# Decoder block on one core: low parts of three gate/up weight operands by a negated copy and an accumulating transfer

## The chip, the core and the metric

The kernel is one program on one NeuronCore of a Trainium2 chip. The core has five engines that run their own instruction streams in order and wait for each other by semaphores: TensorE (PE in the profile; its weight loads are PEld), VectorE (DVE), ScalarE (ACT), GpSimd (POOL) and SyncE (SP). SP, ACT and POOL can issue transfers (DMAs), which then run beside the engines. The metric is the device time of one execution in microseconds (us), smaller being better.

## What is computed

The reference is a decoder layer on an input of 1024 rows by 1024 channels in float32: a mixer (pooling and differential attention), then a gated feed-forward network. Only the feed-forward network matters here:

```python
u = rms_norm(h, ffn_pre_g)
f = silu(u @ w_ffn_gate) * (u @ w_ffn_up)      # 1024 x 2816, called gate/up here
h = h + rms_norm(f @ w_ffn_down, ffn_post_g)   # called down here
```

Two devices shape the kernel. First, each float32 matrix is split into a high part `hi`, which is its value rounded to the type float32r, and a low part `lo = a - hi`; a product is then three matmuls, `hi*hi + hi*lo + lo*hi`. Second, products are made in the manner of Strassen and Winograd: an operand is cut into quarters, sums and differences of the quarters are formed, and seven products of a quarter's size take the place of eight. The operands of the seven products on the weight side are called B11, T1, B21, T2, T3, B22 and T4.

## The kernel before

The program runs through the mixer's projections, attention, the output projection, gate/up and down. In gate/up the 2816 hidden channels are 22 blocks of 128. Blocks 0, 1 and their partners are done one by one; the rest are done as nine *pairs*, `kb` from 2 to 10, block `kb` with block `kb + 11`. Down follows, with `FP = 11` steps for each of its seven products.

**A pair.** `pair_weights(kb)` loads four raw weight tiles of 128x1024 float32 (gate and up, each for the upper and lower half of the channels: `g0`, `u0`, `g1`, `u1`), two transfers of 256 KB each, on SP. It forms T1, T2, T3, T4 in place by `diff` on DVE. Each of the seven operands is then split: `copy` on ACT casts the raw tile to `hi`, and `tt` on DVE makes `lo` as raw minus `hi` (`split`, called by `both`, lines 1418 and 1422 being the DVE and ACT instructions themselves). `outer` keeps an operand whole, `inner` (for B21 and T4) cuts it once more. `pair_products` runs the products in the order of the table `ORDER`: `P1a` is the first product for the pair's first block, `P5b` the fifth (T1) for its second, and `2.1` to `2.7` and `4.1` to `4.7` are the seven small products (128x256 matmuls) in which the second and the fourth product are made. P6 uses T2, P7 uses T3 and P3 uses B22. In a product the line 1920 is `hi*hi`, 1921 is `hi*lo` and 1922 is `lo*hi`, `lo` of the weights being first read in line 1922. ACT copies the results of products 1, 5 and 6 out of the accumulator banks, DVE adds later ones to them, ACT applies silu, DVE multiplies, and SP writes the results to memory (`fsd`).

**What sets the order.** The instructions of this stage aren't issued in the order of the code. `hidden` records them as tasks in a `Plan`, with a cost in us, a rank and the tiles that they read and write. PE's tasks are chained in the given order. `deadlines` gives the others a due time that follows from PE's. `schedule` then fills the engines one task after another by these costs, with limits on the tiles alive (16 of the kind `vr` for `hi` and `lo`, 8 of `vf` for raw tiles), and `emit` issues them in the order of their planned starts. A tile may be claimed by a new user when all users of the old one are done. So a change of one cost or one task can move many others, and the physical tile that a value lands in (its name in the profile: `v`, `Wl`, `Wh`, `F`) differs between versions. `room` says when a task can have the tiles that it needs. Each engine still runs its stream in order on the chip, whatever the plan's costs were.

Of the kernel before, what the change touches and what calls it, by code (L numbers as in the profile page):

```python
# [12 lines left out]
F32R = mybir.dt.float32r  # L13
AF = mybir.ActivationFunctionType
ALU = mybir.AluOpType

P = 128
# [4 lines left out]
HALF = 512  # L22
# [35 lines left out]
class Slot:  # L58


    def __init__(self, pool, make, kind=None, value=None, free_at=None):
        self.pool, self.make, self.kind, self.value = pool, make, kind, value
        self.free_at, self.live, self.left = free_at, value is not None or free_at is not None, 0
        self.log, self.phys, self.first = [], None, None

    def __call__(self):
        return self.value
# [9 lines left out]
class Plan:  # L77
# [84 lines left out]
        return None if s.kind == "own" else self.queues.get(s.kind if s.kind in self.queues else s.pool)  # L162

    def room(self, t):
        need = {}
        for s in t.needs:
            if s.live:
                continue
            q = self.queue(s)
            if q and s not in q[:1 + sum(not x.live and self.queue(x) is q for x in t.needs if x is not s)]:  # L170
                return INF
            if s.pool:
                n, extra = need.get((s.pool, None), (0, 0))
                need[s.pool, None] = n + 1, max(extra, self.own.get(s.pool, 0) if s.kind == "late" else RESERVE.get(s.kind, 0))
                if s.kind in LIMIT:
                    need[s.pool, s.kind] = need.get((s.pool, s.kind), (0, 0))[0] + 1, 0
        at = 0.0
        for (p, kind), (n, extra) in need.items():
            live = [s for s in self.pools[p] if kind is None or s.kind == kind]
            over = len(live) + n + extra - (CAPS[p] if kind is None else LIMIT[kind])  # L180
            if over > 0:
                times = sorted(INF if s.free_at is None else s.free_at for s in live)
                at = max(at, times[over - 1] if over <= len(times) else INF)
        return at

    def schedule(self, patience=None, begin=None):
        patience = patience or {}
        free = {e: (begin or {}).get(e, 0.0) for e in ("PE", "ACT", "DVE", "POOL", "SP")}
        waiting = {t: len(t.before) for t in self.tasks}
        open_ = {e: [] for e in free}  # L190
        dma_free, order, port = 0.0, [], {"DVE": 0.0, "POOL": 0.0}
        for t in self.tasks:
            if not waiting[t]:
                open_[t.engine].append((0.0, t))
        for _ in range(len(self.tasks)):
            best = None
            for e, ts in open_.items():
                f, first = free[e], INF
                cand = []
                for ready, t in ts:  # L200
                    at = max(f, ready, self.room(t), port["POOL" if e == "DVE" else "DVE"] if t.port else 0.0)
                    if at < INF:
                        cand.append((at, t.rank, t))
                        first = min(first, at)
                if not cand:
                    continue
                lim = first + patience.get(e, 0.0) + 1e-9
                at, rank, t = min((c for c in cand if c[0] <= lim), key=lambda c: (c[1], c[0]))
                if best is None or at < best[0]:
                    best = at, t  # L210
            if best is None:
                stuck = [(t.engine, t.rank, [s.pool for s in t.needs if not s.live]) for ts in open_.values() for _, t in ts[:6]]
                raise RuntimeError(f"stuck {stuck} { {p: len(v) for p, v in self.pools.items()} }")
            at, t = best
            e = t.engine
            for s in t.needs:
                if s.pool and not s.live:
                    live = self.pools[s.pool]
                    same = [x for x in live if x.kind == s.kind]
                    if s.kind in LIMIT and len(same) >= LIMIT[s.kind]:  # L220
                        live.remove(min((x for x in same if x.free_at is not None), key=lambda x: x.free_at))
                    elif len(live) >= CAPS[s.pool]:
                        old = min((x for x in live if x.free_at is not None), key=lambda x: x.free_at)
                        live.remove(old)
                        s.phys = old.phys
                    else:
                        s.phys = len(live)
                    live.append(s)
                    if s.kind == "own":
                        self.own[s.pool] -= 1  # L230
                    elif self.queue(s):
                        self.queue(s).remove(s)
                s.live = True
            t.start = at
            if e == "PE" and at > free[e] + 1e-6 and free[e] > 0:
                t.start = at = at + PE_RESTART
            t.end = t.landed = at + t.cost
            if t.port:
                port[e] = t.end
            free[e] = t.end - min(OVERLAP.get(e, 0.0), t.cost / 2)  # L240
            if t.size:
                dma_free = max(dma_free, t.end) + t.size / DMA_RATE if t.size > .01 else dma_free
                t.landed = (dma_free if t.size > .01 else t.end) + DMA_LATENCY
            for s in t.uses:
                s.left -= 1
                if s.pool and not s.left:
                    s.free_at = max(x.landed + self.hop(x, t) for x, _, _ in s.log)
            open_[e] = [(r, x) for r, x in open_[e] if x is not t]
            order.append(t)
            for x in t.after:  # L250
                waiting[x] -= 1
                if not waiting[x]:
                    ready = max(b.landed + self.hop(b, x) for b in x.before)
                    open_[x.engine].append((ready, x))
        self.order = sorted(order, key=lambda t: t.start)
        return max(t.end for t in self.tasks)
# [440 lines left out]
def act(n):  # L697
    return 0.145 + n / 1180
# [10 lines left out]
def mixer(pl, k):  # L709
# [663 lines left out]
    for s in (F, *(t for ts in U2.values() for t in ts), *(t for hi, lo, _ in W2.values() for t in (hi, lo))):  # L1373
# [5 lines left out]
FIRST = {"B21": 2, "T4": 3}  # L1379
ORDER = ("P1a", "4.4", "P1b", "P5a", "2.1", "2.5", "P5b", "2.6", "2.2", "P6a", "2.7", "2.3", "P6b", "2.4", "P7a", "P7b",  # L1380
         "4.1", "4.5", "P3a", "4.6", "4.2", "P3b", "4.7", "4.3")
OUTER = {"1": ("Y", "B11", "A11"), "5": ("X", "T1", "S1"), "6": ("Y", "T2", "S2"), "7": ("Y", "T3", "S3"), "3": ("X", "B22", "S4"),
         "4": ("Y", "T4", "A22")}
INNER = {"1": ("Y", "B11", "A11", 0, 0), "5": ("X", "T1", "S1", 1, 1), "6": ("Y", "T2", "S2", 1, 0), "2": ("Z", "B21", "A12", 0, 0),
         "7": ("Y", "T3", "S3", 1, 1), "3": ("X", "B22", "S4", 1, 0), "4": ("Y", "T4", "A22", 0, 1)}
WRAPPED = ("4.4",)
KEEP_LATE = 10.0


def hidden(pl, k):  # L1390
# [3 lines left out]
    V, A, G = (nc.vector, nc.scalar, nc.gpsimd) if k else (None, None, None)  # L1394
    f32 = k.f32 if k else None
    FP, HQ = NF // 2, HALF // 2
    clock = [0.0]

    def formed(v, dt, shape):
        letters = "abc"[:len(shape)]  # L1400
        return v.rearrange(f"p ({' '.join(letters)}) -> p {' '.join(letters)}", **dict(zip(letters, shape)))

    def v4(dt, *shape):
        s = pl.tile("vr" if dt == F32R else "vf", None)
        s.make = lambda: formed(k.place(s.pool, s.phys), dt, shape)
        return s
# [10 lines left out]
    def tt(o, a, b, op, n, r, w, rank=1e5):  # L1417
        return pl.op("DVE", dve(n), lambda: V.tensor_tensor(out=o(), in0=a(), in1=b(), op=op), r=r, w=w, rank=rank,  # L1418
                     port=all(x.pool not in BANKS for x in slots(r, w)))

    def copy(o, a, n, r, w, rank=1e5, claim=()):
        return pl.op("ACT", act(n), lambda: A.copy(o(), a()), r=r, w=w, rank=rank, claim=claim)  # L1422
# [16 lines left out]
    for names in (("B11", "B21"), ("T1", "T3"), ("T2", "T4"), ("B22",)):  # L1439
        both = [pl.given("vr", k.W[names[0]][j]() if k else 0) for j in range(2)]  # L1440
# [24 lines left out]
    def keep_hidden(kb, q, behind=None):  # L1465
# [6 lines left out]
        def gp(o, a, b, op):  # L1472
            tt(q[o][0], q[a][0], q[b][0], op, HALF, [q[a][1], q[b][1]], [q[o][1]], clock[0] + KEEP_LATE)

# [115 lines left out]
    def pair_weights(kb):  # L1590
# [9 lines left out]
        def both(raw):  # L1600
            hi, lo = v4(F32R, 2, 4, P), v4(F32R, 2, 4, P)
            split(hi, lo, raw, 2 * HALF, [raw], [hi], [lo], claim=[lo])
            return hi, lo

        def outer(n, raw):
            hi, lo = both(raw)
            W[n] = [(hi, lo, e) for e in range(2)]

        def diff(o, a, b):
# [57 lines left out]
    def pair_products(kb, W, q, tail):  # L1667
# [9 lines left out]
        def outer(n, e):  # L1677
            o, w, a = OUTER[n]
            s, key, v = acc[o][e]
# [40 lines left out]
            if len(done) == 26 or (not deep["4"] and "P4b" in done):  # L1720
                keep_hidden(kb, q)

        order = ORDER
        if not deep["4"]:
            order = [x for x in order if x[0] != "4"] + ["P4a", "P4b"]
        for x in order:
# [661 lines left out]
```

## Time and profile before

| | |
|---|---|
| median of 3 runs | 1236.37 us (1236.11 to 1236.63) |
| the profiled execution, device time | 1236.7 us |
| its span, from the first to the last instruction | 1234.8 us |
| ACT busy, share of the span | 606.1 us, 49% |
| POOL busy, share of the span | 59.5 us, 5% |
| DMA bytes moved | 194.43 MB, mean 157 GB/s |

The profiled execution is 0.3 us above the median of the three runs, and 1.9 us of its time lie around its span. The page gives the busy time of each engine, forty slices of the span, the DMA queues, the chain of work that ended last, and the costliest groups of instructions. In a group's row stand the line, the engine, the operation, what it writes and reads, the count, the total busy time and the mean of one in ns, and then the engine's idle time just before, with what ended it. In the timeline, a row is start (us), duration (us), engine, line, operation, tiles, shape and count.

### The profile page before, as it was taken

The numbers are of one execution on the slowest core, as the hardware profiler recorded it, in microseconds if no ns is written. First come the engines' busy times: TensorE is split into PE (matmuls) and PEld (weight loads), VectorE is DVE, ScalarE is ACT, GpSimd is POOL, SyncE is SP. The second block draws the span as 40 slices with busy tenths as digits, with TensorE's granted clock in tenths as the row PEclk, the third lists the DMA queues.
The fourth block names the chain that finished last, engine by engine and source line by source line (L and its number), as shares of the span: only waits on it lengthen the run. The fifth ranks groups of instructions, "written<-read, shape, count | busy, mean of one in ns | idle before, by whom it ended". The sixth has DMA issues, their size and how long they took to land.

```text
span 1234.8 us, 16572 instructions
## 1 busy us (share of the span) xinstructions
PE 1225.1 (99%) x6166; PEld 1042.0 (84%) x6166; DVE 929.2 (75%) x1533; ACT 606.1 (49%) x1098; POOL 59.5 (5%) x64
## 2 busy tenths in 40 slices
PE   9999999999999999999999999999999999999997
PEld 8888888888899998888888888888888888888886
DVE  6986784534599888885877978778878788765666
ACT  8643444443588773454643434434434443644542
POOL 1000000000201110010000000000000000000222
PEclk9999999999999999999999999999999999999999
DMA  9665246323783027672424443223432299533336
GB/s 374 240 194 188 105 158 221 125 80 120 286 327 137 18 85 257 210 267 77 147 97 124 119 128 101 71 94 120 128 128 89 66 319 316 181 103 94 88 101 213
DMA packets 139153, 194.43 MB, mean 157 GB/s; under 512 B 9024, under 2 KB 83520, under 8 KB 138048
## 3 DMA queue, kind: packets, MB, share of 16 engines
q1 hardware_dynamic: 132256, 172.26, 42.1%
q10 hardware_dynamic: 6816, 21.11, 4.4%
q8 instruction: 48, 0.79, 0.3%
q14 instruction: 33, 0.27, 0.1%
HBM read 131.73 MB, written 61.60 MB: 157 GB/s over the span
## 4 chain that ended last, share of the span: by engine, by line
PE 96%; DMA 2%; ACT 1%; DVE 0%; SPq 0%; issue 0%; POOLq 0%; DVEq 0%; ACTq 0%
PE Y L1920 9%; PE Y L1921 9%; PE Y L1922 9%; PE X L1920 5%; PE X L1921 5%; PE X L1922 5%; PE Yd L1921 3%; PE Yd L1922 3%; PE Yd L1920 3%; PE s L731 3%; PE o L731 3%; PE qk L563 3%; PE wo L1920 2%; PE wo L1922 2%; PE wo L1921 2%; PE branch L1920 2%
## 5 line engine op out<-in xcount | busy, mean ns | idle before, releaser
L1827 DVE TENSOR_TENSOR w_op<-wd,w_op 128x512 fp32r<-128x512 f32 x72 | 52.2, 725 | 48.1 <-ACT w_op L1875 48.1
L1418 DVE TENSOR_TENSOR v<-v,v 128x1024 fp32r<-128x1024 f32 (+4 forms) x79 | 73.6, 936 | 9.1 <-ACT v L1422 7.8
L1875 ACT CAST w_op<-wd 128x512 fp32r<-128x512 f32 x72 | 44.8, 623 | 68.0 <-PE Yd L1922 32.1
L1922 PE MATMUL Y<-S_hi,Wl 128*128 128x512 f32 x200 | 77.9, 390 | 0.0
L1922 PE MATMUL X<-S_hi,Wl 128*128 128x512 f32 x200 | 77.8, 389 | 0.0
L1920 PE MATMUL Yd<-w_op,s_op 128*128 128x512 f32 x156 | 60.7, 389 | 0.0
L1921 PE MATMUL Yd<-w_op,s_op 128*128 128x512 f32 x156 | 60.7, 389 | 0.0
L1922 PE MATMUL Yd<-w_op,s_op 128*128 128x512 f32 x156 | 60.7, 389 | 0.0
L1422 ACT CAST v<-v 128x1024 fp32r<-128x1024 f32 (+2 forms) x52 | 42.0, 818 | 36.3 <-PE X L1921 23.7
L1827 DVE TENSOR_TENSOR s_op<-s_raw,s_op 128x512 fp32r<-128x512 f32 x69 | 53.9, 781 | 7.1 <-ACT s_op L1875 7.1
L1875 ACT CAST s_op<-s_raw 128x512 fp32r<-128x512 f32 x69 | 42.6, 617 | 29.6 <-DMA s_raw<-fsd 24.0
L1920 PE MATMUL Y<-A_hi,Wh 128*128 128x512 f32 x144 | 56.2, 390 | 0.0
L1921 PE MATMUL Y<-A_lo,Wh 128*128 128x512 f32 x144 | 56.2, 390 | 0.0
L921 DVE CUSTOM_DVE_ANT_0 E<-s,negd 128x1024 f32<-128x1024 f32 (+7 forms) x64 | 47.4, 748 | 11.4 <-PE s L731 11.3
L1920 PE MATMUL X<-S_hi,Wh 128*128 128x512 f32 x136 | 53.2, 391 | 0.0
L1920 PE MATMUL Y<-S_hi,Wh 128*128 128x512 f32 x136 | 53.1, 390 | 0.0
L1921 PE MATMUL Y<-S_lo,Wh 128*128 128x512 f32 x136 | 53.0, 390 | 0.0
L927 ACT ACTIVATE E<-E,nm 128x1024 f32<-128x1024 f32 (+7 forms) x64 | 49.6, 776 | 6.9 <-DVE nm L921 6.7
L1922 PE MATMUL Y<-A_hi,Wl 128*128 128x512 f32 x136 | 52.9, 389 | 0.0
L1921 PE MATMUL X<-S_lo,Wh 128*128 128x512 f32 x136 | 52.9, 389 | 0.0
L1920 PE MATMUL wo<-woh,mh 128*128 128x512 f32 x128 | 50.5, 394 | 0.0
L1922 PE MATMUL wo<-woh,ml 128*128 128x512 f32 x128 | 49.9, 390 | 0.0
(515 smaller groups left out, 3735.6 us busy)
## 6 DMA issues: line engine op xcount, KB each, us to landing
s_raw<-fsd SPq DMA_DIRECT2D x31, 512.0 KB, 3.7
fsd<-v SPq DMA_DIRECT2D x56, 256.0 KB, 3.5
w_raw<-in_w_in_dram SPq DMA_DIRECT2D x24, 512.0 KB, 4.1
wd<-in_w_ffn_down_dram SPq DMA_DIRECT2D x44, 256.0 KB, 5.2
sgs<-sgd SPq DMA_DIRECT2D x16, 512.0 KB, 8.6
sgd<-g_st ACTq DMA_DIRECT2D x14, 512.0 KB, 4.1
v<-in_w_ffn_up_dram SPq DMA_DIRECT2D x28, 256.0 KB, 4.5
v<-in_w_ffn_gate_dram SPq DMA_DIRECT2D x26, 256.0 KB, 3.4
```

Of the source, the lines that this page charges most:

```text
L563: nc.tensor.matmul(o()[:, cs], l, r, start=first and kk == 2 * kh and j == 0, stop=last and kk == 2 * kh + 1 and j == len(todo) - 1, skip_ ...
L731: nc.tensor.matmul(o, l, r, start=start, stop=stop, skip_group_check=skip)
L921: V.tensor_tensor_reduce(out=view[m]().rearrange("p (j w) -> p j w", j=nj), in0=sc()[:, :nj, :w], in1=negd()[:, S - L:S].rearrange("p (j w ...
L927: A.activation(view[m](), view[m](), AF.Exp, bias=nm()[:, m:m + 1], scale=-1.0, accum_out=sums()[:, m:m + 1])
L1418: return pl.op("DVE", dve(n), lambda: V.tensor_tensor(out=o(), in0=a(), in1=b(), op=op), r=r, w=w, rank=rank, port=all(x.pool not in BANKS ...
L1422: return pl.op("ACT", act(n), lambda: A.copy(o(), a()), r=r, w=w, rank=rank, claim=claim)
L1827: nc.vector.tensor_tensor(out=o, in0=a, in1=f32(hi), op=ALU.subtract)
L1875: nc.scalar.copy(hi, a)
L1920: nc.tensor.matmul(o, ah, bh, start=start, stop=False, skip_group_check=goes_on)
L1921: nc.tensor.matmul(o, ah, bl, start=False, stop=False, skip_group_check=goes_on)
L1922: nc.tensor.matmul(o, al, bh, start=False, stop=stop, skip_group_check=goes_on)
```

## The change

Three things are changed.

1. For the operands B22, T2 and T3 of each pair, `outer` no longer calls `both`. ACT casts raw to `hi` as before. ACT then writes `-hi` into the tile of `lo` (`A.mul` by -1), and POOL issues a transfer from the raw tile to the tile of `lo` that adds to what is there (`accum_op=ALU.add`), so `lo` becomes raw minus `hi`. DVE's subtraction for the three operands goes. B11, T1, B21 and T4 are made as before.
2. The last pair (`kb == FP - 1`) has an order of its own, `ORDER_LAST`: `4.7` stands ahead of `P3b`.
3. In the planner a tile remembers when it was granted (`since`), and a task that uses a granted tile isn't planned ahead of that time.

```diff
-        self.log, self.phys, self.first = [], None, None
+        self.log, self.phys, self.first, self.since = [], None, None, 0.0
...
     def room(self, t):
-        need = {}
+        need, at = {}, 0.0
         for s in t.needs:
             if s.live:
+                at = max(at, s.since)
                 continue
...
-        at = 0.0
         for (p, kind), (n, extra) in need.items():
...
-                s.live = True
+                if not s.live:
+                    s.live, s.since = True, at
...
+ORDER_LAST = (*ORDER[:-3], "4.7", "P3b", "4.3")
...
+SHARED = ("B22", "T2", "T3")
...
         def outer(n, raw):
-            hi, lo = both(raw)
+            if n in SHARED:
+                hi, lo = v4(F32R, 2, 4, P), v4(F32R, 2, 4, P)
+                copy(hi, raw, 2 * HALF, [raw], [hi], claim=[lo])
+                pl.op("ACT", act(2 * HALF), lambda: A.mul(lo(), f32(hi()), -1.0), r=[hi], w=[lo], rank=1e5)
+                pl.op("POOL", 1.0, lambda: G.dma_start(lo(), raw(), accum_op=ALU.add), r=[raw], w=[lo], rank=1e5, size=1.0)
+            else:
+                hi, lo = both(raw)
             W[n] = [(hi, lo, e) for e in range(2)]
...
-        order = ORDER
+        order = ORDER if kb < FP - 1 else ORDER_LAST
```

The streams of all engines are the same up to the first pairs; from there to the end of the pairs they differ. PE has the same 6166 matmuls.

**First place: ACT in the pair kb = 4.** Before, from the copy of P1a's result out of its bank (`COPY v_6073<-Y_6864`) on, with T2's cast (`Wl_5959`), T3's cast (`Wl_5890`) and the two copies of the fifth product (`p_`):

```order
L1422 COPY v_6073<-Y_6864 128x512
L1422 CAST v_6189<-v_6070 128x1024
L1429 ACTIVATE v_6145<-v_6145 128x512
L1422 CAST Wl_5959<-F_5749 128x1024
L1422 CAST v_6098<-v_6017 128x512
L1422 COPY v_6073<-Y_6895 128x512
L1422 CAST v_6098<-v_6017 128x256
L1422 COPY p_1171_6947<-X_6916 128x512
L1422 CAST Wl_5890<-v_6167 128x1024
L1422 COPY p_1174_6995<-X_6916 128x512
L1422 COPY u_1175_7022<-Y_6864 128x512
```

Now, in the same pair, the lines being nine or so higher; `L1612` is the negated copy, of T2 (`Wh_5960`), T3 (`v_6051`) and B22 (`v_6076`):

```order
L1612 ACTIVATE Wh_5960<-Wl_5959 128x1024
L1432 ACTIVATE v_6017<-v_6017 128x512
L1425 COPY F_5749<-Y_6870 128x512
L1425 CAST Wl_5941<-v_6017 128x1024
L1432 ACTIVATE v_6017<-v_6017 128x512
L1425 CAST v_6075<-v_6070 128x1024
L1425 COPY F_5749<-Y_6904 128x512
L1612 ACTIVATE v_6051<-v_6075 128x1024
L1425 COPY p_1171_6956<-X_6924 128x512
L1425 CAST Wl_5890<-F_5749 128x1024
L1425 COPY p_1174_6997<-X_6924 128x512
L1612 ACTIVATE v_6076<-Wl_5890 128x1024
```

T2's operand now stands ahead of the copy of P1a, T3's ahead of P5a's copy (`p_1171`), and B22's just behind P5b's (`p_1174`); before, T3's cast stood behind P5a's copy and B22's behind the first copy of the sixth product. POOL, which had nothing in this stage, issues the transfers, three to a pair in the order T2, T3, B22; those of this pair and the next begin with:

```order
L1613 DMA Wh_5960<-v_6073 128x1024
L1613 DMA v_6051<-v_6070 128x1024
L1613 DMA v_6076<-F_5749 128x1024
L1613 DMA Wh_5924<-v_6017 128x1024
L1613 DMA Wh_5942<-v_6073 128x1024
```

**Second place: who takes the raw tiles over.** T2's raw tile in this pair is `v_6073` and T3's is `v_6070`. SP now loads the next pair's `up` weights into them, with the writes of results (`fsd`) between:

```order
L1435 DMA v_6073<-in_w_ffn_up_dram 128x4x128
L1435 DMA fsd<-v_6167 128x512
L1435 DMA v_6073<-in_w_ffn_up_dram 128x4x128
L1435 DMA fsd<-v_6167 128x512
L1435 DMA fsd<-v_6017 128x512
L1435 DMA v_6070<-in_w_ffn_up_dram 128x4x128 x2
L1435 DMA v_6167<-in_w_ffn_gate_dram 128x4x128 x2
```

DVE then subtracts the two (`v_6073<-v_6070,v_6073`, the next pair's T3), and behind that stand the last quarter of T4 of this pair, the addition of `2.4` (`Yi_6948`), T4's `lo` (`Wh_5960<-v_6145,Wl_5959`), P7a's addition and B11's `lo` of the next pair:

```order
L1421 TENSOR_TENSOR v_6073<-v_6070,v_6073 128x1024
L1421 TENSOR_TENSOR v_6145<-v_6145 128x256
L1421 TENSOR_TENSOR F_5749<-F_5749,Yi_6948 128x256
L1421 TENSOR_TENSOR v_6145<-v_6145 128x256
L1421 TENSOR_TENSOR Wh_5960<-v_6145,Wl_5959 128x1024
L1421 TENSOR_TENSOR p_1171_6956<-Y_6870,p_1171_6956 128x512
```

So a raw tile is handed on to a load when the accumulating transfer out of it has landed, where before it was handed on at the end of DVE's subtraction.

**Third place: PE in the last pair.** Before, `4.2` (`Zi`) was followed by P3b (`X`):

```order
L1921 MATMUL Zi_8971<-A_hi_5653,v_6098 128x256
L1922 MATMUL Zi_8971<-A_hi_5653,v_6097 128x256
L1920 MATMUL X_8740<-S_hi_5816,v_6075 128x512
L1921 MATMUL X_8740<-S_lo_5852,v_6075 128x512
L1922 MATMUL X_8740<-S_hi_5816,Wh_5942 128x512
```

Now it is followed by two matmuls of down (`Yd`) and by `4.7` (`Yi`), behind which P3b stands:

```order
L1930 MATMUL Zi_8998<-A_lo_5666,Wh_5891 128x256
L1931 MATMUL Zi_8998<-A_hi_5653,v_6098 128x256
L1929 MATMUL Yd_9070<-Wh_5924,Wl_5890 128x512
L1930 MATMUL Yd_9070<-Wh_5924,Wl_5890 128x512
L1929 MATMUL Yi_8957<-v_6097,v_6076 128x256
L1930 MATMUL Yi_8957<-v_6097,v_6076 128x256
L1931 MATMUL Yi_8957<-v_6097,v_6188 128x256
```

`4.7` adds to the bank that `4.6` used, so it has to wait until DVE has added `4.6`'s result; P3b, 12 matmuls, no longer stands between the two.

## The prediction

> **What bounds the kernel now.** I read the page first: the span, the busy times, and the chain of work that ended last.
>
> ```profile
> span 1234.8 us, 16572 instructions
> PE 1225.1 (99%) x6166; PEld 1042.0 (84%) x6166; DVE 929.2 (75%) x1533; ACT 606.1 (49%) x1098; POOL 59.5 (5%) x64
> PE 96%; DMA 2%; ACT 1%; DVE 0%; SPq 0%; issue 0%; POOLq 0%; DVEq 0%; ACTq 0%
> ```
>
> PE is busy 1225.1 of 1234.8 us and makes 96% of the chain; the two shares agree. All that any change of the other engines can take away is 9.7 us of idle PE, wherever it lies. So the next view is the busy time by stretches: the products before the pairs, the pairs, and from there to the last matmul.
>
> ```profile
> core 0: us, PE busy (x) PEld busy (x) DVE busy (x) ACT busy (x) POOL busy (x), PEclk, DMA share, GB/s
> 615.00:715.00 100.00, 100.00 (x463) 83.58 (x462) 79.57 (x113) 43.92 (x65) 0.00 (x0) 1.00 0.36 114
> 715.00:1015.00 300.00, 300.00 (x1627) 260.62 (x1626) 246.16 (x403) 126.89 (x193) 0.00 (x0) 1.00 0.38 124
> 1015.00:1228.00 213.00, 213.00 (x949) 176.69 (x949) 151.61 (x240) 98.38 (x189) 22.68 (x19) 1.00 0.51 160
> ```
>
> From 615 to 1228 us PE isn't idle at all, at a granted clock of 1.00. DVE is busy 246 of 300 us in the pairs: high, but below 300, and the reader should see that PE is full beside it. Then the list of PE's waits over the whole span:
>
> ```profile
> PE qk L563 <- ACT A_hi L479: 1.6, 3, 0.8
> PE warm L339 <- POOL ident masks.py:199: 1.4, 1, 1.4
> PE branch L1920 <- DVE sgs L734: 0.3, 1, 0.3
> ```
>
> It has three entries, 3.3 us in all, and none is of the gate/up products (lines 1920 to 1922 with X, Y, Z, Xi, Yi, Zi). In the stage that is changed there is no PE wait to remove. A busy share hides small gaps, since a matmul's end is modelled; but the quoted starts below follow each other at 0.23 us, without a hole.
>
> **What is removed.** Nine pairs lose three subtractions each, 27 on DVE; ACT gains 27 passes over 128x1024. The rows of such instructions, by shape, in the pairs:
>
> ```profile
> L1418 DVE TENSOR_TENSOR Wl<-v,Wl 128x1024 fp32r<-128x1024 f32 x10 | 12.2, 1218 | 0.0
> L1422 ACT CAST v<-v 128x1024 fp32r<-128x1024 f32 x21 | 22.0, 1050 | 8.7 <-PE X L1922 3.3 <-PE Y L1921 3.0 <-PE Xi L1922 0.8
> ```
>
> DVE: 27 x 1.22 = 32.9 us less, 246 to about 213 of 300 us. On the path it is worth 0: PE waited for no DVE instruction here, so what is late next is PE itself, as before. ACT: the negated copy isn't in the trace; the cast of the same tile (1.05 us) is the nearest row, bounded below by nothing and above by twice that. 27 x 1.05 = 28.4 us more, 127 to about 155 of 300. It is covered by ACT's idle half, but the place counts, since each copy stands ahead of or behind a copy out of a bank. The rows of the pair kb = 4:
>
> ```profile
> 758.93 0.59 ACT L1422 COPY v<-Y 128x512 f32<-128x512 f32 x1 [1.16 <-PE Y L1922]
> 765.11 0.59 ACT L1422 COPY p<-X 128x512 f32<-128x512 f32 x1 [1.66 <-PE X L1922]
> 770.02 0.58 ACT L1422 COPY p<-X 128x512 f32<-128x512 f32 x1
> ...
> 771.00 0.39 PE L1922 MATMUL Y<-S_hi,Wh 128*128 128x512 f32 x1
> 778.64 0.39 PE L1922 MATMUL Y<-S_hi,Wl 128*128 128x512 f32 x1
> 784.35 0.28 PE L1920 MATMUL Xi<-A_hi,v 128*128 128x256 f32 x1
> 785.54 0.39 PE L1922 MATMUL X<-S_hi,Wh 128*128 128x512 f32 x1
> ```
>
> Ahead of P1a's copy ACT was idle for 1.16 us and ahead of P5a's for 1.66, so a pass of 1.05 fits; were P1a's copy late by 1 us, nobody would see it, since its bank is next used by P6a, 12 us on. I take 0.
>
> **What is added: a transfer in the operand's path.** By the order now, the copies for T2, T3 and B22 are done by P1a's copy (758.93), by P5a's (765.11), and 1.05 us behind the end of P5b's (770.02 + 0.58 + 1.05 = 771.65). The first matmuls that read these low parts are the line 1922 rows of P6a (771.00), P7a (778.64) and P3a (785.54). So the windows, from the start on POOL to the need, are **12.1, 13.5 and 13.9 us**. The trace has no accumulating transfer and no transfer from POOL. The nearest rows, by size and by engine:
>
> ```profile
> s_raw<-fsd SPq DMA_DIRECT2D x31, 512.0 KB, 3.7
> vd<-v_st ACTq DMA_DIRECT2D x4, 1024.0 KB, 4.4
> V<-vd SPq DMA_DIRECT2D x4, 1024.0 KB, 10.6
> v<-in_w_ffn_up_dram SPq DMA_DIRECT2D x28, 256.0 KB, 4.5
> ...
> L855 POOL TENSOR_TENSOR wb_lo<-wb_raw,wb_hi 128x1024 fp32r<-128x1024 f32 x4 | 10.1, 2524 | 60.3 <-ACT wb_hi L853 60.3
> L1091 POOL TENSOR_TENSOR rstd<-ms,mhalf 128x1 f32<-128x1 f32 x16 | 9.6, 599 | 128.4 <-DVE ms L1095 118.0 <-DVE ms L1099 10.4
> ```
>
> It writes 512 KB and reads two operands of 512 KB. From below: POOL's smallest instruction, 0.6, and a 512 KB landing, 3.7, in all 4.3 us. From above: POOL over a whole 128x1024 tile, 2.5, and the slowest landing of 1,024 KB, 10.6, in all 13.1. I take 1.5 for POOL's part, midway, and 4.4 for the landing, because the row `vd<-v_st` also reads 1,024 KB out of the core's own memory and runs at a moderate load, as here (DMA share 0.38): **about 6 us**. That is half the shortest window, so PE doesn't wait: 0 us. POOL has nothing else in this stage, so nothing is queued behind its waits but the next transfer, 6 us later.
>
> **What is moved: the raw tile is released later.** Before, the next load could follow DVE's subtraction; now it follows the landing. The place that decides is T3's raw tile: landing, then two loads on SP, then DVE's difference for the next pair, and in DVE's queue behind that T4's low part, which `4.5` (784.35) needs. The rows for the terms that aren't quoted yet:
>
> ```profile
> 799.40 0.94 SPq L1432 DMA_DIRECT2D F<-in_w_ffn_gate_dram  x2
> ...
> 1012.45 0.28 PE L1920 MATMUL Yi<-Wh,v 128*128 128x256 f32 x1
> 1013.37 0.42 DVE L1418 TENSOR_TENSOR v<-v,Yi 128x256 f32<-128x256 f32 x1
> ```
>
> Issue 0.9, landing 4.5, difference 1.22, three small DVE instructions 3 x 0.42, T4's cast 1.05 and subtraction 1.22 make 10.15 us. T3's transfer starts by 765.11, and 784.35 - 765.11 - 10.15 = **9.1 us** is what it may take. Six is less: 0 us. SP's other work behind those loads is writes of results, which nobody waits for in this stage.
>
> **The last pair.** Between `4.6` and `4.7`, which adds to the same bank, now stand `4.2` (0.72) and two matmuls of down (0.45), 1.17 us in place of 3.4. DVE's addition of `4.6` ended at 1013.79, 0.62 after the product's last issue slot (1012.45 + 0.72). If DVE is in a 0.7 us instruction just then, PE waits some 0.2 us. I take 0; at most 0.7.
>
> **The sum.** 1236.7 (the profiled execution, 1234.8 of span and 1.9 around it) - 0 + 0 + 0 + 0 = 1236.7, and for the median, which lay 0.3 lower, **1236.4 us**.
>
> **The rivals.**
>
> *The raw tiles come late (slower).* If the transfer takes more than 9.1 us from POOL's start, DVE stands at the next pair's difference, and each of the eight pairs that have a next one loses the excess, since T3's start is tied to PE's own progress by P5a. At 10.5 us that is 8 x 1.4 = 11 us, 1248; at the upper bound of 13.1, 8 x 4.0 = 32, 1268. For it: three transfers a pair are added to a DMA share of 0.38, and 10.6 us is on record for 1,024 KB. Against it: 4.4 is on record too. 9%.
>
> *POOL can't start while DVE runs (slower).* DVE's work in the pairs comes in long stretches without idle time, for example between these two rows, of which each tells the idle time before it:
>
> ```profile
> 798.14 1.22 DVE L1418 TENSOR_TENSOR v<-F,v 128x1024 fp32r<-128x1024 f32 x1 [0.63 <-ACT v L1422]
> 807.45 0.42 DVE L1418 TENSOR_TENSOR v<-v,Yi 128x256 f32<-128x256 f32 x1 [0.64 <-PE Yi L1922]
> ```
>
> That stretch is 807.45 - 0.64 - 798.14 = 8.7 us. If POOL had to sit it out, 6 us would become 14.7, the raw tiles would be 5.6 us late, and 8 x 5.6 = 45 us would give 1281. If POOL gets its turn after one instruction (1.22 us), 6 becomes 7.2 and nothing is seen. Nothing in the trace speaks for it, since POOL was idle in the pairs. 6%. The Trainium skill, "SBUF — State Buffer", section "SBUF: two separate sides", warns of this case: a transfer issued from POOL has its descriptors written by GpSimd's cores, which DVE's two-port operations lock out of the port pair they share. By that rule the time would be between 1236 and 1281, by how many instructions it waits; by the rows alone it is 1236.4. The same section ties the lock to two-port modes, and "Advanced Engine Details and Errata", section "Instruction Support", lists none for tensor_tensor, DVE's only kind of instruction in the quoted rows; no run here shows a POOL transfer beside DVE yet.
>
> *One early wait (no measurable change).* In the first deep pairs DVE forms the quarters of A22 in a raw tile that T3 of kb = 3 gives up, with additions for PE queued behind. Such a wait happens once; between 8 and 9.1 us of transfer it costs about 1 us, 1237.5. 7%.
>
> *Faster.* The change does relieve DVE, but its gain needs a PE wait to remove. Inside the pairs there is none, and outside nothing is moved. More than 2.5 us could only come from matmuls that run quicker, of which no row gives a sign. 3%, at 1233.
>
> **How the numbers follow.** The forecast, no change, has 75%: 1235.8 to 1237.0, the spread of the runs before (0.5 us) and some tenths for the last pair. A measurement of this kernel can tell about 0.2%, 2.5 us, from no change. Same: 75 + 7 and 1 from the mildest late tiles, 83%. Slower: the rest of the two rivals, 14%. Faster: 3%. The range runs from 1235.4 to 1239.5: it takes in the forecast, the early wait and late tiles up to 0.4 us a pair, and leaves out some 13% above and 3% below. The rivals above reach far, but with little chance.
>
> **What would show it.** DVE's busy time lower by about 33 us and ACT's higher by about 28 say that the exchange is as costed. 27 transfers from POOL with about 6 us from issue to landing, and an empty list of PE waits between 615 and 1228 us, say that it is hidden. PE waits on Y or X at line 1922 would mean that the transfer itself is late; on Xi or Yi at line 1920, with DVE waiting for a `v<-in_w_ffn_up` load or for a POOL transfer, that the raw tiles are. POOL instructions of more than 3 us would speak for the rival of DVE's stretches. The prediction is wrong if the transfer takes over 9 us in the steady pairs, or if PE's matmuls change their pace.

## The result, and the profile after

| | before | changed |
|---|---|---|
| median | 1236.30 us (4 runs, 1236.11 to 1236.63) | 1252.88 us (4 runs, 1251.30 to 1255.63) |
| ratio, 95% interval | 1 | 1.0136, 1.0116 to 1.0157 |
| profiled execution, its span | 1236.7, 1234.8 us | 1254.09, 1252.3 us |

The changed kernel is slower by 16.6 us. The forecast of 1236.4 us was wrong, and so was its range, which ended at 1239.5. In the rows of the changed kernel the lines of DVE, ACT and SP (1418, 1422, 1429, 1432 before) are three higher, not nine as said above; 1920 to 1922 are 1929 to 1931. The page of the changed kernel has, for the rows shown of before:

```profile
span 1252.3 us, 16690 instructions
...
PE 1231.2 (98%) x6166; PEld 1045.6 (83%) x6166; DVE 897.7 (72%) x1506; ACT 635.3 (51%) x1125; POOL 83.2 (7%) x91
...
PE 89%; DVE 4%; DMA 4%; issue 2%; ACT 1%; SPq 0%; DVEq 0%; POOLq 0%; ACTq 0%
...
L1421 DVE TENSOR_TENSOR v<-v,v 128x1024 f32<-128x1024 f32 (+3 forms) x43 | 43.8, 1023 | 22.7 <-DMA v<-in_w_ffn_up_dram 9.6
...
L1929 PE MATMUL X<-S_hi,Wl 128*128 128x512 f32 x100 | 40.8, 408 | 9.7 <-DVE u L1421 9.7
```

The exchange is as costed: DVE 31.5 us less, ACT 29.2 more. But the span grew by 17.5 us: PE's idle time rose from 9.7 to 21.1 us, by 11.4, and its busy time, for the same 6166 matmuls, by 6.1. The chain that ended last now has DVE in it with 4% (0% before) and DMA with 4% (2%). The last two rows say where: DVE stands before the differences of weights (`v<-v,v`) for loads, and PE stands before P3b (`X`, line 1929 now) for DVE's addition into `u`. The stretches and PE's waits say the same:

```profile
core 0: us, PE busy (x) PEld busy (x) DVE busy (x) ACT busy (x) POOL busy (x), PEclk, DMA share, GB/s
615.00:715.00 100.00, 100.00 (x463) 83.58 (x462) 74.95 (x108) 47.54 (x67) 3.71 (x4) 1.00 0.47 134
715.00:1015.00 300.00, 287.93 (x1530) 248.03 (x1529) 201.67 (x348) 140.68 (x197) 20.15 (x23) 0.99 0.54 141
```

```profile
PE X L1929 <- DVE u L1421: 11.1, 7, 2.1
...
PE Xi L1931 <- DVE Wh L1421: 0.8, 1, 0.8
PE Xi L1929 <- ACT Wl L1425: 0.2, 1, 0.2
```

Columns: who waited for whom, us in total, times, longest. Seven waits of P3b, 11.1 us in all, once in each of the pairs kb = 3 to 9; the pair kb = 10, which has no next one, has none. The waits on Xi are `4.5` in kb = 9, for T4's low and high part. The list has no entry for a low part that POOL's transfer makes: the transfer itself never keeps PE waiting here. What does is seen in one pair, kb = 5, engine by engine; the pairs kb = 4 to 9 are alike (kb = 3, with 0.4 us, comes another way, see "One early wait" below). First POOL (T2, T3, B22), then SP, DVE and PE:

```profile
800.12 0.87 POOL L1613 DMA_DIRECT2D Wh<-v  x1 [27.02 <-DVE v L1421]
806.53 0.87 POOL L1613 DMA_DIRECT2D Wh<-v  x1 [5.54 <-ACT Wh L1612]
813.43 0.89 POOL L1613 DMA_DIRECT2D v<-v  x1 [6.03 <-ACT v L1612]
```

```profile
815.21 1.74 SPq L1435 DMA_DIRECT2D v<-in_w_ffn_up_dram  x2
```

```profile
816.15 1.23 DVE L1421 TENSOR_TENSOR F<-v,v 128x1024 f32<-128x1024 f32 x1 [3.54 <-DMA fsd<-F]
...
820.48 1.23 DVE L1421 TENSOR_TENSOR v<-v,v 128x1024 f32<-128x1024 f32 x1 [0.84 <-DMA v<-in_w_ffn_up_dram]
...
824.02 1.23 DVE L1421 TENSOR_TENSOR Wh<-v,Wl 128x1024 fp32r<-128x1024 f32 x1 [1.30 <-ACT Wl L1425]
825.16 0.69 DVE L1421 TENSOR_TENSOR p<-Y,p 128x512 f32<-128x512 f32 x1
825.76 1.22 DVE L1421 TENSOR_TENSOR Wh<-v,Wl 128x1024 fp32r<-128x1024 f32 x1
826.89 0.69 DVE L1421 TENSOR_TENSOR p<-Y,p 128x512 f32<-128x512 f32 x1
...
827.82 1.22 DVE L1421 TENSOR_TENSOR v<-v,F 128x1024 f32<-128x1024 f32 x1
828.96 1.22 DVE L1421 TENSOR_TENSOR Wh<-F,Wl 128x1024 fp32r<-128x1024 f32 x1
...
830.42 1.22 DVE L1421 TENSOR_TENSOR F<-F,v 128x1024 f32<-128x1024 f32 x1
831.56 0.68 DVE L1421 TENSOR_TENSOR u<-X,u 128x512 f32<-128x512 f32 x1
```

```profile
830.59 0.28 PE L1931 MATMUL Zi<-A_hi,v 128*128 128x256 f32 x1
832.30 0.50 PE L1929 MATMUL X<-S_hi,v 128*128 128x512 f32 x1 [1.43 <-DVE u L1421]
```

T3's transfer starts at 806.53. SP's next two loads go into its raw tile and are issued at 815.21, right behind its landing: 8.6 us, as the DMA view of that instant says (what moved, the queue, how many, KB, us from the start to the landing).

```profile
Wh<-v POOLq DMA_DIRECT2D x1, 512.0 KB, 8.6
```

DVE's difference for the next pair waits for the second load (820.48). T4's low part follows at 824.02 and is in time for `4.5`. But behind it in DVE's queue stand P7a's addition, B11's low part, P7b's addition, two differences and T1's low part, and only then, 7.54 us later, P3a's addition (831.56). P3b accumulates into the tile of banks that this addition reads, and waits for it: it starts at 832.30 where it could have at 830.71. Before, in the same pair, P3a's addition had waited for PE itself and was done half a microsecond ahead of P3b:

```profile
825.45 0.69 DVE L1418 TENSOR_TENSOR u<-X,u 128x512 f32<-128x512 f32 x1 [0.37 <-PE X L1922]
```

```profile
826.57 0.28 PE L1922 MATMUL Zi<-A_hi,v 128*128 128x256 f32 x1
826.69 0.40 PE L1920 MATMUL X<-S_hi,v 128*128 128x512 f32 x1
```

The load isn't the only thing that holds DVE. Some 4 us ahead of the difference another one had waited 3.54 us for a result write out of the tile that it takes over (816.15). In DVE's waits between 715 and 1015 us, where the list of before has none for a DMA, such writes are the first entry:

```profile
DVE v L1421 <- DMA fsd<-v: 16.4, 5, 3.9
...
DVE v L1421 <- DMA v<-in_w_ffn_up_dram: 7.8, 4, 3.6
```

The two writes issued next to T3's transfer landed with it, 8 us after their issue. Take DVE's wait for the load off P3b's delay, and what is left in kb = 5 is 1.59 - 0.84 = some 0.7 us; in kb = 4, 6, 7 and 8 it is 0.4 to 1.1. By this estimate the late writes alone would have cost that much.

### The profile page after: what moved, and what is told of

Same layout as the page of the kernel before. It is cut to its first block, busy times and chain, and to the rows that moved or that the text cites. A ratio compares the mean times of both kernels' runs of the same rounds, so it can differ in the third digit from the quotient of the medians.

```text
span 1252.3 us, 16690 instructions
## 1 busy us (share of the span) xinstructions
PE 1231.2 (98%) x6166; PEld 1045.6 (83%) x6166; DVE 897.7 (72%) x1506; ACT 635.3 (51%) x1125; POOL 83.2 (7%) x91
## 4 chain that ended last, share of the span: by engine, by line
PE 89%; DVE 4%; DMA 4%; issue 2%; ACT 1%; SPq 0%; DVEq 0%; POOLq 0%; ACTq 0%
PE Y L1929 8%; PE Y L1930 8%; PE Y L1931 8%; PE X L1929 5%; PE X L1930 5%; PE X L1931 4%; PE Yd L1931 3%; PE Yd L1930 3%; PE Yd L1929 3%; PE s L732 3%; PE o L732 3%; PE qk L564 3%; PE branch L1929 2%; PE branch L1931 2%; PE branch L1930 2%; PE wo L1931 2%
## 5 line engine op out<-in xcount | busy, mean ns | idle before, releaser
L1425 ACT CAST Wl<-v 128x1024 fp32r<-128x1024 f32 (+2 forms) x54 | 44.5, 827 | 62.6 <-PE X L1930 43.8
L1421 DVE TENSOR_TENSOR v<-v,v 128x1024 f32<-128x1024 f32 (+3 forms) x43 | 43.8, 1023 | 22.7 <-DMA v<-in_w_ffn_up_dram 9.6
L1931 PE MATMUL X<-S_hi,Wl 128*128 128x512 f32 x152 | 59.1, 389 | 0.0
L1929 PE MATMUL X<-S_hi,Wh 128*128 128x512 f32 x144 | 56.3, 391 | 0.0
L1930 PE MATMUL X<-S_lo,Wh 128*128 128x512 f32 x144 | 56.0, 389 | 0.0
L922 DVE CUSTOM_DVE_ANT_0 E<-s,negd 128x1024 f32<-128x1024 f32 (+7 forms) x64 | 47.4, 749 | 11.4 <-PE s L732 11.3
L1931 PE MATMUL Y<-S_hi,Wl 128*128 128x512 f32 x136 | 53.0, 390 | 0.0
L1929 PE MATMUL X<-S_hi,Wl 128*128 128x512 f32 x100 | 40.8, 408 | 9.7 <-DVE u L1421 9.7
```

The source lines that it names most:

```text
L922: V.tensor_tensor_reduce(out=view[m]().rearrange("p (j w) -> p j w", j=nj), in0=sc()[:, :nj, :w], in1=negd()[:, S - L:S].rearrange("p (j w ...
L1929: nc.tensor.matmul(o, ah, bh, start=start, stop=False, skip_group_check=goes_on)
L1930: nc.tensor.matmul(o, ah, bl, start=False, stop=False, skip_group_check=goes_on)
L1931: nc.tensor.matmul(o, al, bh, start=False, stop=stop, skip_group_check=goes_on)
```

## Experiments

Twelve kernels, in three groups; the texts of the expectations speak of theories H (the raw tile is handed on too late), C (contention of bytes) and O (the new order alone). The kernel before, run beside them, had medians of 1236.33 us (small, small_traffic, traffic, none_shared), 1236.41 (late_t3, small_then_traffic, t2_b22, plan_longer) and 1236.21 (the other four). In the diffs, `...` stands for what is left out.

| run | median, us | ratio to before, 95% interval |
|---|---|---|
| small | 1238.29 | 1.0015, 1.0005 to 1.0024 |
| small_traffic | 1253.34 | 1.0144, 1.0120 to 1.0168 |
| traffic | 1241.05 | 1.0037, 1.0024 to 1.0050 |
| none_shared | 1236.26 | 1.0000, 0.9991 to 1.0010 |
| late_t3 | 1273.38 | 1.0292, 1.0266 to 1.0318 |
| small_then_traffic | 1239.06 | 1.0021, 1.0012 to 1.0030 |
| t2_b22 | 1249.04 | 1.0101, 1.0079 to 1.0122 |
| plan_longer | 1238.90 | 1.0018, 1.0008 to 1.0028 |
| half | 1241.39 | 1.0043, 1.0028 to 1.0058 |
| t2_only | 1236.22 | 1.0000, 0.9990 to 1.0009 |
| t3_only | 1236.56 | 1.0004, 0.9995 to 1.0013 |
| plan_3 | 1245.78 | 1.0078, 1.0063 to 1.0093 |

**small.** The transfer is kept, its bytes go.

```diff
-                pl.op("POOL", 1.0, lambda: G.dma_start(lo(), raw(), accum_op=ALU.add), r=[raw], ...
+                pl.op("POOL", 1.0, lambda: G.dma_start(lo()[:, 0, 0, :32], raw()[:, 0, 0, :32], accum_op=ALU.add), r=[raw], ...
```

> The changed kernel with each accumulating transfer cut to 128x32 elements; all engines keep the changed kernel's order, row for row. Left out: the other 992 columns of the low parts of T2, T3 and B22 keep the negated copy. Theory H (the raw tile is handed on too late: T3's transfer lands 8.3 to 9.1 us after POOL's start, the next pair's difference on DVE waits for the load behind it, and P3a's addition stands behind that in DVE's queue): a transfer of 16 KB lands in 2 to 4 us, the PE waits on X at P3b vanish, 1236 to 1239 us. Theory C (contention: 14 MB more of traffic slow SP's loads and writes): the traffic is gone, 1236 to 1239. Theory O (the new order of DVE's queue alone is too tight, whatever the transfer does): the PE waits at P3b stay at 1.5 to 2 us a pair, 1249 to 1254.

1238.29 us: 14.6 of the 16.6 us are gone, with every other instruction in the same order. O falls as the main cause, but not wholly. PE still loses 0.28 us at P3b:

```profile
826.77 0.28 PE L1931 MATMUL Zi<-A_hi,v 128*128 128x256 f32 x1
827.06 0.50 PE L1929 MATMUL X<-S_hi,v 128*128 128x512 f32 x1
827.40 0.39 PE L1930 MATMUL X<-S_lo,v 128*128 128x512 f32 x1
```

The starts are 0.29 and 0.34 apart where 0.12 and 0.23 are usual, together 0.28. The six pairs kb = 4 to 9 lose that much and kb = 3 0.18, in all 1.8 us, nearly all of this run's excess of 2.0. From P7b's addition, which waits for PE, to P3a's DVE has no idle time: the new order has no slack left there. T3's transfer of 16 KB still took 5.7 us in the same pair.

**small_traffic.** The bytes come back, beside the small transfer.

```diff
+                pl.op("POOL", 0.0, lambda: G.dma_start(scrap().rearrange(...), f32(hi()), accum_op=ALU.add), r=[hi], rank=1e5)
```

> As the run with transfers of 128x32, with the full traffic put back beside it: behind each small transfer POOL issues an accumulating transfer of 512 KB from the operand's high part to a spare tile that nobody reads, so no raw tile and no low part waits for it. Order of PE, DVE, ACT and SP as in the changed kernel. H: the raw tiles are handed on early, so at most a few tenths a pair, 1236 to 1240. C: the writes of results and the loads are as slow as in the changed kernel, DVE waits for them, 1245 to 1254. O: 1249 to 1254.

1253.34 us looks like C, but the run doesn't tell the two apart. POOL issued the 512 KB transfer first and the small one 0.7 us behind it; the DMA view of those two issues, one after the other, has:

```profile
junk<-Wl POOLq DMA_DIRECT2D x1, 512.0 KB, 7.1
```

```profile
Wh<-v POOLq DMA_DIRECT2D x1, 16.0 KB, 7.0
```

The small transfer landed 0.6 us after the large one. So the raw tile was handed on late here too, and the loads behind it were slow as well (the table under `half`).

**small_then_traffic.** The same, with the 512 KB transfer reading the low part, so that it is issued behind the small one (`f32(lo())`, `r=[lo]`).

> As the run with small transfers and full traffic, with the order on POOL turned round: the transfer of 512 KB to the spare tile reads the low part, so it is issued behind the small one and the small one doesn't stand behind it in the queue. H: T3's small transfer lands some 6 us from POOL's start as without traffic, the load behind it takes 1 to 2 us longer, which the difference has to spare: 1238 to 1242. C: the same bytes in the same places slow loads and writes as in the changed kernel, 1246 to 1254.

1239.06 us, in H's range. All the bytes are there, and they cost at most 0.8 us over `small`, which the two intervals don't tell apart; PE's only waits at P3b are two of 0.2 us. The bytes come some microseconds later than in the changed kernel, so they meet other neighbours.

**late_t3.** No bytes, but T3's operand gets three small transfers in a chain.

```diff
+                def add():
+                    for _ in range(3 if n == "T3" else 1):
+                        G.dma_start(lo()[:, 0, 0, :32], raw()[:, 0, 0, :32], accum_op=ALU.add)
+                pl.op("POOL", 1.0, add, r=[raw], ...
```

> As the run with transfers of 128x32, but T3's operand gets three of them in a chain, each behind the landing of the one before: no traffic, and T3's raw tile is handed on late. All other engines keep the changed kernel's order. Left out: most of the three low parts, as there. In the run with small transfers T3's landed 5.7 us from POOL's start, the next pair's difference had 1.9 us to spare behind its load, and DVE about 0.8 us in all behind that. H: the time is that run's 1238.3 plus seven pairs times what the landing exceeds 8.4 us from the first start; for a landing at 10 us 1249, at 12 us 1263, with PE waits on X at P3b of that size. C: no bytes are added, 1238 to 1239.

1273.38 us, with next to no traffic: late hand-on makes such waits without the bytes. In the pairs kb = 5 to 8 the chain took 10.3 to 10.5 us, for which the formula has some 2.0 us a pair, and PE's waits are that:

```profile
PE X L1932 <- DVE u L1421: 12.2, 6, 2.1
PE Y L1934 <- DMA Wh<-v: 6.2, 1, 6.2
PE Yi L1932 <- DVE v L1421: 5.4, 1, 5.4
```

The total misses (1253 by the formula at 10.5): the two other waits, one in kb = 3 and one in the last pair, there for the low part itself, and matmuls that ran slowly behind the waits (below) weren't foreseen.

**half.** The transfer moves half of each tile (`lo()[:, 0]`, `raw()[:, 0]`).

> The changed kernel with each accumulating transfer cut to half the tile, 256 KB; all engines in the changed kernel's order. Left out: the other half of the three low parts keeps the negated copy. T3's transfer landed 5.7 us from POOL's start with 16 KB and 8.6 with 512 KB. H, with a landing that grows with the bytes: 7.1 us, which is below the 8.4 from which the difference is late, so 1238 to 1240. If instead any transfer of size queues as the full one does (landing above 8 us), 1246 to 1254.

The landing was as expected, the time 1.4 us above the range. The DMA view at T3's issue in kb = 5 has 7.2 us for 256 KB; PE's waits at P3b are small, six of 3.8 us in all. Over the pairs kb = 4 to 9 the landings, in us from POOL's start, order by size and by place:

| | 16 KB | 256 KB | 512 KB |
|---|---|---|---|
| T2, first of the pair | 2.0 to 3.4 | 3.3 to 4.3 | 4.7 to 5.4 |
| T3, second | 5.3 to 5.8 | 7.0 to 7.4 | 8.3 to 9.1 |

So the bytes of a whole tile add some 3 us at either place, and T3's place adds some 3.5 at any size.

Hand-on and bytes meet in one sum, T3's landing and from there to the landing of the second load. In kb = 5, in us, for the runs that keep the changed kernel's order:

| | T3's landing | to the second load's | sum | P3b late |
|---|---|---|---|---|
| small | 5.7 | 3.9 | 9.6 | 0.2 |
| small_then_traffic | 5.8 | 4.8 | 10.6 | 0.2 |
| half | 7.2 | 5.6 | 12.8 | 0.5 |
| the changed kernel | 8.6 | 5.2 | 13.8 | 1.6 |
| small_traffic | 7.0 | 6.9 | 13.9 | 1.6 |
| late_t3 | 10.5 | 4.1 | 14.5 | 2.2 |

Where P3b is late by more than the 0.2 us of the order, its delay is this sum less 12.2 to 12.3. So neither H nor C is the cause alone in the changed kernel: with the 3.9 us of `small` behind it, a landing of 8.6 would make 12.5 and a delay of some 0.3 us, by estimate, where 1.6 were measured.

**traffic.** The kernel before in its own order, with 27 transfers of 512 KB for which nobody waits.

```diff
+            if n in ("B22", "T2", "T3"):
+                pl.op("POOL", 1.0, lambda: G.dma_start(scrap().rearrange(...), f32(hi()), accum_op=ALU.add), r=[hi], rank=1e5)
```

> The kernel before, with its own order row for row (low parts by DVE's subtraction), and 27 accumulating transfers of 512 KB from the high parts of T2, T3 and B22 to a spare tile that nobody reads. H: nothing waits for them, 1236 to 1237.5. C: loads and writes land later by 1 us and more and PE waits come, 1240 to 1250. O: the order is the old one, 1236 to 1237.5. Landing of SP's result writes in this stage: 3.5 us before, 4.5 in the changed kernel; if that is the transfers' doing, 4.3 to 5 here.

1241.05 us: C is right that bytes cost, 4.7 us here. PE waits at two P3b, 2.4 us in all, and DVE now waits for loads between 715 and 1015 us, where the list of before has no wait for a DMA:

```profile
DVE v L1418 <- DMA F<-in_w_ffn_up_dram: 7.6, 2, 4.5
DVE F L1418 <- DMA v<-in_w_ffn_up_dram: 7.3, 2, 4.3
DVE v L1418 <- DMA v<-in_w_ffn_up_dram: 6.0, 2, 3.1
```

The median landing of the 256 KB loads of `up` into `v` between 715 and 1015 us was 4.2 us before, 5.1 in the changed kernel and 6.1 here. The Trainium skill, "DMA: Bandwidth & Descriptors", section "Issuing engines are not separate DMA queues", says that transfers of all issuing engines run on the same 16 DMA engines; POOL's transfers slowing SP's loads agrees.

**none_shared.** `SHARED = ()`, the rest of the change kept.

> The changed kernel with the list of the three operands empty: all low parts by DVE again, while the last pair's own order and the planner's memory of when a tile was granted stay. H, C and O all put the cost on the three operands: 1236 to 1237. A fourth possibility, that the other two parts of the change cost something: above 1238.5.

1236.26 us. The last pair's order and the planner's memory cost nothing.

**t2_b22, t2_only, t3_only.** `SHARED = ("B22", "T2")`, `("T2",)` and `("T3",)`; the order is planned anew in each.

> The changed kernel with T3's low part by DVE's subtraction again and T2's and B22's by the accumulating transfer. H: T3's raw tile is handed on by DVE, as before, so the loads behind it start early; T2's and B22's transfers land about 5 us from POOL's start: 1236.5 to 1239. C: two thirds of the added bytes remain, so about two thirds of the 16.6 us, 1244 to 1249.

> The changed kernel with T2 alone by the transfer, T3 and B22 by DVE. T2's transfer is the first of a pair and landed 4.9 to 5.4 us from POOL's start, ahead of the loads and result writes. H: its raw tile is handed on in time, 1236.3 to 1238. If every transfer costs by its bytes, a third of 16.6 us: 1241 to 1243.

> The changed kernel with T3 alone by the transfer. It stands among the next pair's loads and four result writes, so it lands 7 to 8.6 us from POOL's start though it is the only one. H: 1240 to 1250, with the PE waits behind a difference on DVE that waits for a load. If every transfer costs by its bytes: 1241 to 1243, as T2 alone.

One transfer a pair is free, whichever of the two: 1236.22 and 1236.56. That speaks against "a cost by bytes", a third of the loss for each operand. For T3 alone H's 1240 to 1250 missed too, but its transfer was quicker than expected: in the pairs kb = 4 to 9 it landed in 6.2 to 7.1 us (8.8 only in the last pair, which has no next one), so this run doesn't test a late hand-on. T2 and B22 without T3 cost 12.6 us, at the upper end of what C had (1244 to 1249), and H as I had put it, with T3's tile as the place, can't explain it. The trace of t2_b22, DVE and PE:

```profile
853.13 1.23 DVE L1421 TENSOR_TENSOR v<-F,v 128x1024 f32<-128x1024 f32 x1 [2.69 <-DMA fsd<-v]
...
856.20 1.23 DVE L1421 TENSOR_TENSOR F<-F 128x1024 f32<-128x1024 f32 x1 [1.50 <-DMA F<-in_w_ffn_up_dram]
857.34 1.22 DVE L1421 TENSOR_TENSOR Wh<-v,Wl 128x1024 fp32r<-128x1024 f32 x1
```

```profile
858.61 0.50 PE L1931 MATMUL Y<-S_hi,Wh 128*128 128x512 f32 x1 [2.11 <-DVE Wh L1421]
```

It is the same mechanism at another product. Again DVE first waits for a result write (853.13), then for a load (856.20). The second transfer of a pair, now B22's, is the late one (9.4 us from 842.77), the loads behind it are issued at 852.24, the next pair's difference waits for them, and behind it in DVE's queue stands the low part that PE needs, here T3's. So the place is not T3's tile but the raw tile whose next load feeds a difference ahead of something that PE needs.

**plan_longer, plan_3.** The same instructions; the planner counts the transfer as 2.0 or 3.0 MB (`size=`), so it expects the landing 2.6 or 5.3 us later.

> The changed kernel with one number of the planner changed: it counts the accumulating transfer as 2.0 in place of 1.0 MB, so it plans the landing 2.6 us later and the loads around it later too. The instructions are the same, their order is not. H with the queue on DVE as its second half: the planner, knowing of the late tile, places the next pair's difference behind P3a's addition or other work, and the stalls shrink: 1237 to 1246. C: the traffic is the same, 1248 to 1254 whatever the order.

> The changed kernel with the planner counting the transfer as 3.0 MB in place of 1.0 (2.0 gave 1238.9, of which one wait in the pair kb = 3 made 2 us and the later pairs nothing). H: the later pairs stay free, and the total depends on whether an early wait is left: 1236.3 to 1239.5. It can't beat the kernel before by more than 0.3 us, since PE was full there.

At 2.0: 1238.90 us. The transfers still take up to 8.7 us, the bytes are all there, yet from kb = 4 on PE doesn't wait: the planner has moved the difference, as DVE's rows in kb = 6 show:

```profile
857.52 1.23 DVE L1421 TENSOR_TENSOR Wh<-v,v 128x1024 fp32r<-128x1024 f32 x1 [1.30 <-ACT v L1425]
858.66 0.68 DVE L1421 TENSOR_TENSOR p<-Y,p 128x512 f32<-128x512 f32 x1
859.27 1.22 DVE L1421 TENSOR_TENSOR v<-F,Wl 128x1024 fp32r<-128x1024 f32 x1
860.40 1.22 DVE L1421 TENSOR_TENSOR v<-v 128x1024 f32<-128x1024 f32 x1
```

It stands (860.40) behind T4's low part (857.52) and P7a's addition, no longer ahead of them, and waits for no load. What is left is in kb = 3, at `4.3`, about 2 us. At 3.0, 1245.78 us and above the range, the later pairs are free as well, and the loss is again in kb = 3, larger and earlier, at `4.6`:

```profile
755.95 0.58 PE L1929 MATMUL Yi<-Wh,v 128*128 128x256 f32 x1 [5.84 <-DVE v L1421]
```

No version beat the kernel before; t2_only and t3_only equal it, as is to be expected where PE is full.

## Why the prediction was wrong, point by point

- **What bounds the kernel, and DVE's relief at 0:** right. With one operand DVE loses 9 subtractions and the time is 1236.22.
- **ACT's extra passes at 0, POOL able to start beside DVE:** right. PE has one wait of 0.2 us for ACT in the pairs. POOL's 27 instructions took 0.86 to 1.08 us each, though DVE was busy 202 of 300 us. T2's transfer in kb = 5, which was quick, ran while DVE was busy 4.89 of 6 us (800 to 806), T3's, which was slow, while it was busy 2.76 of 10 (806 to 816). The Trainium skill, "SBUF — State Buffer", section "SBUF: two separate sides", warns that DVE's two-port operations hold up a transfer issued from POOL; besides them it names operations with two inputs in SBUF, but only against a GpSimd operation that reads SBUF, which the prediction left out. These rows show no sign of either.
- **The transfer, "about 6 us":** mis-sized where it counted. The median of the 27 was 5.7, but T3's took 8.3 to 9.1 in kb = 4 to 9. The landing had been taken at the stage's mean DMA share of 0.38. At the place where T3's transfer would stand, the trace of before had more than twice that, a row that the prediction didn't read (columns as above; the last two are DMA share and GB/s):

```profile
765.00:775.00 10.00, 10.00 (x63) 8.98 (x62) 7.83 (x16) 2.88 (x5) 0.00 (x0) 1.00 0.82 260
```

- **The raw tile's allowance, "9.1 us":** this is the step that failed, together with the size of the transfer. The chain, T3's landing, two loads, the difference, T4's low part, was the right one for `4.5`: 9.1 for the transfer and 5.4 for issue and landing of the loads are 14.5 us, and `4.5` was on time in all pairs but kb = 9, where they took 15.9. But the queue was followed only to the first thing that PE needs. P3a's addition, 7.54 us further back, had less time, 12.2 us by the table under `half`, which with the 5.4 leaves 6.8 for the transfer in place of 9.1. It took both errors: 6 + 5.4 = 11.4 us would have been in time for P3a's addition, and 8.6 + 5.4 = 14.0 for `4.5`.
- **The result writes, "which nobody waits for":** this failed too. It held before; in the changed kernel DVE waits for one in each of the pairs kb = 4 to 9, 2.9 to 3.9 us, ahead of the load.
- **The rival "the raw tiles come late":** it happened, with a chance of 9%. Its form was right, a loss in the pairs with a next one (six here, kb = 4 to 9). PE's place was not Xi or Yi but X, and the price was wrong: by its 9.1 us, transfers of 8.3 to 9.1 would have cost nothing, where P3b was late by 11.7 us in the six pairs.
- **"One early wait":** it happened as well, with a chance of 7%. In kb = 3 DVE waits 4.40 us for T3's transfer (at 728.52, the first addition for A22's quarters), and P3b is 0.5 us late behind it; no load is waited for there. In late_t3 the same wait of DVE is 11.6 us, and PE waits 5.4.
- **The last pair at 0:** right; none_shared has its order and loses nothing.

The sum as it came out, by the starts of the same matmuls in the traces of none_shared and of the changed kernel: P3b starts late by 12.3 us in all, `4.5` in kb = 9 by 1.5, the second matmul of P3b each time by another 0.1, 0.7 in all, and slow matmuls behind two waits cost 3.2 (last section); together some 17.6, where the spans differ by 17.9. Shown by experiment: that late hand-on alone can make the waits (late_t3), that the bytes placed behind the hand-on hardly do (small_then_traffic), and that another order hides the same transfers (plan_longer). Not separated: how much of the loss in kb = 4 to 8 would have come by the result writes alone, and what it is at T3's place that adds 3.5 us at any size.

## What to carry to other kernels

When work moves from an engine to a transfer, ask first when the source buffer is handed on, and read the DMA share at the very place of the transfer, not the stage's mean. Follow the in-order queue behind the waiting instruction to its end, to every item that the bounding engine needs, and take the smallest slack: the first item can be on time and the fifth late. And a planner that fills queues by assumed costs must be given the cost under load: here one number of it was worth 14 us, and raising it once more (plan_3) lost 7 again.

## What the runs showed of the hardware that was not expected

A PE wait of some 2 us can cost 1.6 us extra. Behind the wait at 789.4 (2.07 us beyond the usual start) the matmuls start 0.43 us apart in place of 0.23, at half the granted clock:

```profile
791.57 0.50 PE L1929 MATMUL X<-S_hi,Wl 128*128 128x512 f32 x1 [1.91 <-DVE u L1421]
791.91 0.57 PE L1930 MATMUL X<-S_lo,Wl 128*128 128x512 f32 x1
792.27 0.63 PE L1931 MATMUL X<-S_hi,v 128*128 128x512 f32 x1
792.70 0.63 PE L1929 MATMUL X<-S_hi,Wl 128*128 128x512 f32 x1
```

```profile
791.90:794.90 3.00, 3.00 (x9) 2.34 (x8) 0.88 (x2) 0.00 (x0) 0.00 (x0) 0.51 0.23 87
```

Some eight matmuls at 0.2 us more make 1.6 us, twice in the profiled execution of the changed kernel, 3.2 us; the second time (the wait that ends at 992.0) they begin 1.6 us behind the wait. It isn't every such wait, and not the longest: those that begin at 869.7 and 909.4, of 2.10 and 2.01 us, had none behind them; in small_traffic one of 1.98 us had and two of 2.24 had not. What decides isn't shown. The Trainium skill, "TensorE: Matmul & The Clock Gate", section "Why this matters for your kernels", warns of gaps above about 3 us; here 2.07 sufficed, and 1.98 in small_traffic.

A transfer of 16 KB isn't quick for being small: 2.0 us from POOL's start with little beside it, 5.3 to 5.8 among loads and writes, and 7.0 behind 512 KB on the same queue (small_traffic, kb = 5).
